# A decoder layer on one core: the first stage's work on two engines is given a written order, and three small pieces move

## The chip, the cores and the metric

One core of a Trainium2 chip runs the whole program. The metric is device time in microseconds (us) of one execution. The engines are TensorE (PE in the profile, its weight loads PEld), VectorE (DVE), ScalarE (ACT), GpSimd (POOL) and SyncE (SP), which issues most of the transfers.

## The reference, cut to what matters

One layer runs over 1024 prompt positions and 64 sample positions (T = 1088 columns here), with 1024 features. What the change touches is the beginning:

```python
h = rmsnorm(x, g1)              # x * rsqrt(mean(x*x) + EPS) * g1
proj = h @ w_in                 # 1024 x 2824
u, v, bgate, cgate, hb, z, xbc, dt_raw = jnp.split(proj, cuts, axis=-1)
conv_out, conv_new = causal_dwconv(cgate * hb, conv_prev, conv_w)
xbc_c, sconv_new = causal_dwconv(xbc, sconv_prev, sconv_w, sconv_b)   # then silu
dt = jax.nn.softplus(dt_raw + dt_bias)
```

Behind it come three token mixers, an output projection, and a feed-forward block of 4096 hidden features, `x + relu(rmsnorm(x) @ w_ff1)**2 @ w_ff2`, which is most of the matrix work.

## The kernel before

Features lie on the 128 partitions and tokens in the columns. `xT` is 8 tiles `xt` of 128 x 1088. Products are taken in float32r, with each operand split in a rounded part (high) and a rest (low); `mm3` (L125) adds high x high, low x high and high x low. A weight tile `whl` (128 x 2 x 1024) is made by `split_w` (L94) out of a loaded tile `wst`: ScalarE writes the high part (L97), VectorE the low part (L98). Both pools have two buffers, so the third weight tile takes the buffer of the first. `next_w` (L114) hands out tile i, splits tile i+1 and loads tile i+2.

The first stage goes over the 8 tiles `xt` as they land (L247). For each k, `dt_products` (L240) issues 12 small matmuls of `xt` with the eight dt columns of the weights, into the PSUM tile `psd`. Then the high part of x * g1 is written to `big` (L254 on ScalarE for k > 2, L256 on VectorE for the others), the low part by VectorE (L259), the square of `xt` by ScalarE (L229, `square`, in place but for k = 0), and the squares are summed into `ss` on VectorE (L233, `add_square`). TensorE runs the products of the first weight tile (L333, L337; `w0`) on these parts as they come, into three PSUM tiles `gps`, all that this pool has. The norm's factor 1/rms isn't known by then: it is multiplied onto the results afterwards.

When `w0` is done, ScalarE copies its three PSUM tiles to the buffer `buf` (L342) and `psd` to `dtT` (L344, L345). The second weight tile's products follow (L322, `gemm` with L128 to L130): its first third goes to a PSUM tile `aps` of another pool, so that it need not wait for those copies, and behind that third stands `rms_scale` (L155): three matmuls that sum `ss` over the partitions (L169), a logarithm and an exponential on ScalarE (L170, L174), and a Newton step on VectorE (L177 to L180) that gives `rstd`. Then VectorE multiplies the second tile's results by `rstd` (L290, `evac_pad`), the first tile's by `rstd` (L351), and `dtT` by `rstd` (L355, L357), and the convolutions follow (`conv_c`: L304 on ScalarE, three L307 on VectorE, L309 on ScalarE). Between the thirds of the third weight tile's products stand the small matmuls `dt_tokens` (L379) that turn `dtT` over.

Each engine works its own instructions in the order in which they stand in its program. That order is made by the framework's planner: it runs its own estimate of the program in time, and takes among the instructions that it holds for ready the one that was written first. Within `tc.manual_schedule(engines={...})` (used here at the end, L1346) the engines named keep to the written order instead; engines not named stay with the planner.

Of the kernel before, what the change touches and what calls it, by code (L numbers as in the profile page):

```python
# [7 lines left out]
F32 = mybir.dt.float32  # L8
F32R = mybir.dt.float32r
BF16 = mybir.dt.bfloat16  # L10
AF = mybir.ActivationFunctionType
ALU = mybir.AluOpType
# [3 lines left out]
P = 128  # L16
D = 1024
KT = D // P
# [4 lines left out]
T = SEQ + TS  # L23
# [36 lines left out]
HC = (0, 256, 1024)  # L60
# [8 lines left out]
def body(nc, tc, I, O):  # L69
    ctx = ExitStack()  # L70
    V, S, G, PE, SY = nc.vector, nc.scalar, nc.gpsimd, nc.tensor, nc.sync
# [11 lines left out]
    big = bigp.tile([P, KT * 2 * T], F32R, name="big")  # L83

    def C(name):
        o, n = PCOLS[name]
        return cp[:, o:o + n]
# [3 lines left out]
        SY.dma_start(out=st, in_=src)  # L91
        return st

    def split_w(st, cuts=(0, 1024), pool=None):  # L94
        w = (pool or whlp).tile([P, 2, 1024], F32R, name="whl")
        for a, b in zip(cuts, cuts[1:]):
            S.copy(out=w[:, 0, a:b], in_=st[:, a:b])  # L97
            V.tensor_tensor(out=w[:, 1, a:b], in0=st[:, a:b], in1=w[:, 0, a:b].bitcast(F32),  # L98
                            op=ALU.subtract)
        return w  # L100
# [5 lines left out]
    def w_load(i):  # L106
        if i < len(w_plan) and i not in w_st:
            w_st[i] = load_w(w_plan[i])

    def w_split(i):  # L110
        if i < len(w_plan) and i not in w_sp:
            w_sp[i] = split_w(w_st[i], HC if i == 0 else (0, 1024))

    def next_w():  # L114

# [111 lines left out]
    def square(k):  # L227
        xt = xts[k][:, :T]
        S.activation(out=ss if k == 0 else xt, in_=xt, func=AF.Square)  # L229

    def add_square(k):
        if k > 0:
            V.tensor_tensor(out=ss, in0=ss, in1=xts[k][:, :T], op=ALU.add)  # L233
# [6 lines left out]
    def dt_products(k):  # L240

        parts = [(j, 0, DTQ, j * DTQ) for j in range(4)] + [(j, DTQ, 32, SEQ + 32 * j) for j in range(2)]
        for j, o, n, t in parts:
            PE.matmul(psd[32 * j:32 * j + 32, o:o + n], wdt[:, k], xts[k][:, t:t + n],
                      start=k == 0 and o == 0, stop=k == KT - 1, skip_group_check=True)

    for k in range(KT):  # L247
        xt = xts[k]
        dt_products(k)
        b = big[:, k * 2 * T:(k + 1) * 2 * T].rearrange("p (h t) -> p h t", h=2)  # L250
        g = C("g1")[:, k:k + 1]
        for a, e in (((0, 364), (364, T)) if k == 0 else ((0, T),)):
            if k > 2:
                S.activation(out=b[:, 0, a:e], in_=xt[:, a:e], func=AF.Identity, scale=g)  # L254
            else:
                V.tensor_scalar(out=b[:, 0, a:e], in0=xt[:, a:e], scalar1=g, scalar2=None, op0=ALU.mult)  # L256
        if k == 0:
            w_split(0)
        V.scalar_tensor_tensor(out=b[:, 1], in0=xt[:, :T], scalar=g, in1=b[:, 0].bitcast(F32),  # L259
                               op0=ALU.mult, op1=ALU.subtract)  # L260
        if k:
            square(k - 1)
        if k > 2:
            add_square(k - 2)
        xg.append(b)
    w_split(1)
    square(KT - 1)
    add_square(KT - 2)
    add_square(KT - 1)

    def evac_mul(c, ps, dst, rhs=None):
        rhs = rstd if rhs is None else rhs
# [3 lines left out]
    def pad_parts(buf, pad, src, c):  # L276

        c0, n = CH[c]
        if c < 2:
            return [(buf[:, pad + c0:pad + c0 + n], src[:, :n], lambda a: a[:, c0:c0 + n])]  # L280
        m, w = SEQ - c0, NJ + pad
        sb = buf[:, pad + SEQ:pad + SEQ + NB * w].rearrange("p (b w) -> p b w", w=w)
        rows = lambda a: a.rearrange("p (b w) -> p b w", w=NJ)
        return [(buf[:, pad + c0:pad + SEQ], src[:, :m], lambda a: a[:, c0:SEQ]),
                (sb[:, :, pad:], rows(src[:, m:n]), lambda a: rows(a[:, SEQ:T]))]
# [3 lines left out]
        for o, i, tok in pad_parts(buf, pad, ps, c):  # L289
            V.tensor_tensor(out=o, in0=i, in1=tok(rhs), op=ALU.mult)  # L290

    S.copy(out=ones, in_=C("ones"))
    stC = sml.tile([P, 8, 27], F32, name="stC")
    xcS = sml.tile([P, 8, TS], F32, name="xcS")
    mids = {}
# [44 lines left out]
    for c in range(3):  # L340
        for o, i, tok in pad_parts(buf, 3, ps0[c], c):
            S.copy(out=o, in_=i)  # L342
    dtT = tmpp.tile([P, T], F32, name="dtT", tag="t")[:, :DTQ + 32]
    S.copy(out=dtT[:, :DTQ], in_=psd[:, :DTQ])  # L344
    S.copy(out=dtT[:64, DTQ:], in_=psd[:64, DTQ:DTQ + 32])  # L345
    buf5 = new_buf(3, C("sst")[:, 5 * 24:6 * 24])
    gemm(next_w(), xg, range(KT), lambda c, ps: evac_pad(c, ps, buf5, 3),
         first=ap.tile([P, 512], F32, name="aps", tag="a"), hooks=[lambda: rms_scale(aslots(), catp, "yb", ss, rstd, D, False)])
    for c in range(3):
        for o, i, tok in pad_parts(buf, 3, ps0[c], c):  # L350
            V.tensor_tensor(out=o, in0=o, in1=tok(rstd), op=ALU.mult)  # L351
    conv_c(4, buf)
    for j in range(4):
        r = slice(32 * j, 32 * j + 32)
        V.tensor_tensor(out=dtT[r, :DTQ], in0=dtT[r, :DTQ], in1=rstd[r, j * DTQ:(j + 1) * DTQ], op=ALU.mult)  # L355
        if j < 2:
            V.tensor_tensor(out=dtT[r, DTQ:], in0=dtT[r, DTQ:], in1=rstd[r, SEQ + 32 * j:SEQ + 32 * j + 32],  # L357
                            op=ALU.mult)
    conv_c(5, buf5)


# [95 lines left out]

    stB = sml.tile([P, 2, 18], F32, name="stB")
    catB = []
    V.tensor_tensor(out=ss, in0=rstd, in1=rstd, op=ALU.mult)  # L460

    def proj_b(i):
        cg = tmpp.tile([P, T], F32, name="cg", tag="t")
# [1152 lines left out]
```

## Time and profile before

| | |
|---|---|
| median of 3 runs | 1127.13 us (1126.9 to 1127.19) |
| profiled execution, its own time | 1127.05 us |
| its span, first to last instruction | 1125.3 us |
| TensorE matmul busy | 1111.0 us, 99% of the span, 8524 matmuls |
| VectorE busy | 840.4 us, 75% |
| ScalarE busy | 497.8 us, 44% |
| GpSimd busy | 53.2 us, 5% |

Busy times are unions of the recorded spans of instructions. A matmul's recorded end is modelled, and neighbours overlap, so what a matmul costs is better read from start to start. An idle time in square brackets is what lies ahead of an instruction on its engine, with what ended it.

### The profile page before, as it was taken

Reading aid. Unit: us, or ns where it says so; the run is one execution under the profiler, and the core shown is the slowest. Engines: PE = TensorE matmul, PEld = TensorE weight load, DVE = VectorE, ACT = ScalarE, POOL = GpSimd, SP = SyncE. Lnnn points to the kernel's source line nnn. Section 1 sums busy time; section 2 is a strip of 40 time slices with the busy share of each in tenths; the row PEclk is TensorE's granted clock in tenths of the full one; section 3 lists DMA queues with packets and bytes.
Section 4 is the critical chain, followed back from the end, with each engine's and each line's share of the span. In section 5 each row is a group of like instructions: output and inputs, shape, how many; then the busy total and the mean of one; then the engine's idle time right before and its main releaser. Section 6 shows DMA issues by size and latency. Waiting matters only on the chain.

```text
span 1125.3 us, 19943 instructions
## 1 busy us (share of the span) xinstructions
PE 1111.0 (99%) x8524; PEld 1090.8 (97%) x8524; DVE 840.4 (75%) x1111; ACT 497.8 (44%) x659; POOL 53.2 (5%) x89
## 2 busy tenths in 40 slices
PE   8999999999999999999999999999999999999996
PEld 6999999999999999999999999999999999999995
DVE  8875587865655477999697497596596596599786
ACT  7536273423553344653343443443443442543544
POOL 1110021110000000000000000000000000000014
PEclk9999999999999999999999999999999999999999
DMA  6112233321027263692853953953953953953504
GB/s 257 52 60 62 61 113 104 114 70 52 34 93 280 79 229 117 277 410 80 336 175 129 399 180 138 390 185 138 394 180 144 382 186 146 378 183 142 215 1 160
DMA packets 34776, 200.43 MB, mean 178 GB/s; under 512 B 4736, under 2 KB 7680, under 8 KB 27776
## 3 DMA queue, kind: packets, MB, share of 16 engines
q1 hardware_dynamic: 32592, 196.30, 47.2%
q10 hardware_dynamic: 2096, 2.85, 0.7%
q8 instruction: 67, 1.10, 0.4%
q14 instruction: 21, 0.17, 0.0%
HBM read 175.58 MB, written 22.77 MB: 176 GB/s over the span
## 4 chain that ended last, share of the span: by engine, by line
PE 94%; DVE 3%; issue 1%; ACT 1%; DMA 1%; POOL 0%; SPq 0%; POOLq 0%; DVEq 0%; ACTq 0%
PE ps L1045 20%; PE ps L1044 20%; PE ps L1046 20%; PE gps L128 10%; PE gps L129 9%; PE gps L130 9%; PE aps L574 1%; PE aps L578 1%; DMA xt<-xT 1%; DVE big L259 1%; DVE xq L909 0%; PE aps L509 0%; PE aps L505 0%; PE p L1044 0%; PE aps L767 0%
## 5 line engine op out<-in xcount | busy, mean ns | idle before, releaser
L1045 PE MATMUL ps<-big,whl 128*128 128x272 f32 x1312 | 377.7, 288 | 0.0
L1044 PE MATMUL ps<-big,whl 128*128 128x272 f32 x1312 | 377.5, 288 | 0.0
L1046 PE MATMUL ps<-big,whl 128*128 128x272 f32 x1312 | 376.9, 287 | 0.0
L1045 PEld LDWEIGHTS ps<-big,whl 128*128 128x128 f32 x1312 | 247.1, 188 | 0.2 <-issue 0.2
L1044 PEld LDWEIGHTS ps<-big,whl 128*128 128x128 f32 x1312 | 247.1, 188 | 0.2
L1046 PEld LDWEIGHTS ps<-big,whl 128*128 128x128 f32 x1312 | 246.8, 188 | 0.0
L128 PE MATMUL gps<-big,whl 128*128 128x360 f32 (+2 forms) x752 | 239.8, 319 | 0.5 <-ACT cb L342 0.5
L129 PE MATMUL gps<-big,whl 128*128 128x360 f32 (+2 forms) x752 | 236.8, 315 | 0.5 <-DVE whl L98 0.5
L130 PE MATMUL gps<-big,whl 128*128 128x360 f32 (+2 forms) x752 | 236.0, 314 | 0.0
L97 ACT CAST whl<-wq 128x1024 fp32r<-128x1024 f32 x92 | 96.6, 1051 | 220.7 <-PE ps L1046 132.9
L98 DVE TENSOR_TENSOR whl<-wq,whl 128x1024 fp32r<-128x1024 f32 x92 | 112.3, 1220 | 50.1 <-ACT whl L97 50.1
L128 PEld LDWEIGHTS gps<-big,whl 128*128 128x128 f32 x752 | 141.4, 188 | 2.0 <-ACT cb L342 1.0
L129 PEld LDWEIGHTS gps<-big,whl 128*128 128x128 f32 x752 | 141.4, 188 | 1.1 <-DVE whl L98 0.7
L130 PEld LDWEIGHTS gps<-big,whl 128*128 128x128 f32 x752 | 141.3, 188 | 0.1
L944 DVE TENSOR_TENSOR x<-x,ps 128x544 f32<-128x544 f32 x188 | 130.5, 713 | 7.8 <-PE ps L1046 6.7
L1046 PE MATMUL ps<-fo,whl 128*128 128x272 f32 x416 | 119.5, 287 | 0.0
L1044 PE MATMUL ps<-fo,whl 128*128 128x272 f32 x416 | 119.3, 287 | 0.0
L1045 PE MATMUL ps<-fo,whl 128*128 128x272 f32 x416 | 119.2, 287 | 0.0
L97 ACT CAST whl<-wst 128x1024 fp32r<-128x1024 f32 (+2 forms) x39 | 40.1, 1027 | 129.5 <-PE gps L130 81.0
L1044 PEld LDWEIGHTS ps<-fo,whl 128*128 128x128 f32 x416 | 78.3, 188 | 0.2 <-issue 0.2
L1046 PEld LDWEIGHTS ps<-fo,whl 128*128 128x128 f32 x416 | 78.2, 188 | 0.0
L1045 PEld LDWEIGHTS ps<-fo,whl 128*128 128x128 f32 x416 | 78.2, 188 | 0.0
(327 smaller groups left out, 1382.1 us busy)
## 6 DMA issues: line engine op xcount, KB each, us to landing
big<-xcd SPq DMA_DIRECT2D x47, 2176.0 KB, 9.7
wq<-w SPq DMA_DIRECT2D x66, 512.0 KB, 4.5
xcd<-big SPq DMA_DIRECT2D x7, 2176.0 KB, 8.1
wst<-w_in SPq DMA_DIRECT2D x21, 512.0 KB, 3.6
wst<-w_out SPq DMA_DIRECT2D x16, 512.0 KB, 3.6
x<-xT SPq DMA_DIRECT2D x8, 544.0 KB, 5.4
dec<-scr SPq DMA_DIRECT2D x8, 512.0 KB, 4.1
xt<-xT SPq DMA_DIRECT2D x7, 544.0 KB, 9.0
```

What stands on the lines that cost most here:

```text
L97: S.copy(out=w[:, 0, a:b], in_=st[:, a:b])
L98: V.tensor_tensor(out=w[:, 1, a:b], in0=st[:, a:b], in1=w[:, 0, a:b].bitcast(F32), op=ALU.subtract)
L128: PE.matmul(ps[:, :n], hi, xh, start=start, stop=False)
L129: PE.matmul(ps[:, :n], lo, xh, start=False, stop=False)
L130: PE.matmul(ps[:, :n], hi, xl, start=False, stop=stop)
L259: V.scalar_tensor_tensor(out=b[:, 1], in0=xt[:, :T], scalar=g, in1=b[:, 0].bitcast(F32), op0=ALU.mult, op1=ALU.subtract)
L574: PE.matmul(yps[hh * HD:(hh + 1) * HD, i * L:(i + 1) * L], w[:, h * HD:(h + 1) * HD], m[:, h], start=i == 0 and n == 0, stop=n == len(term ...
L578: PE.matmul(sps[:, g * 256:(g + 1) * 256], bt[:, g * P:(g + 1) * P], xw[:, g * 256:(g + 1) * 256], start=True, stop=True)
L944: V.tensor_tensor(out=out, in0=a, in1=b, op=o)
L1044: PE.matmul(o, hi, xh, start=start and k == 0, stop=False, skip_group_check=True)
L1045: PE.matmul(o, lo, xh, start=False, stop=False, skip_group_check=True)
L1046: PE.matmul(o, hi, xl, start=False, stop=k == ks - 1, skip_group_check=True)
```

## The change

The loop over k becomes three functions, `high`, `low` and the old `square`/`add_square`, called from one block in which VectorE and ScalarE keep to the written order; TensorE, GpSimd and SyncE stay with the planner. Within the block all sums of squares but the first (which is a write) stand behind the last low part, the split of the second weight tile stands behind the first of these sums, and at the end of the block come the load and the split of the third weight tile and the two copies of `psd` to `dtT`. The first weight tile is split in the same two pieces as before, at written places. The copy of `ones` moves behind the first tile's PSUM copies. `dtT` times `rstd` moves ahead of the first tile's multiplication by `rstd` and its convolution. `ss = rstd * rstd`, which is first read by the products of mixer B (L274), moves from VectorE to ScalarE as a Square.

```diff
@@ -91,8 +91,9 @@
         SY.dma_start(out=st, in_=src)
         return st
 
-    def split_w(st, cuts=(0, 1024), pool=None):
-        w = (pool or whlp).tile([P, 2, 1024], F32R, name="whl")
+    def split_w(st, cuts=(0, 1024), pool=None, w=None):
+        if w is None:
+            w = (pool or whlp).tile([P, 2, 1024], F32R, name="whl")
         for a, b in zip(cuts, cuts[1:]):
             S.copy(out=w[:, 0, a:b], in_=st[:, a:b])
             V.tensor_tensor(out=w[:, 1, a:b], in0=st[:, a:b], in1=w[:, 0, a:b].bitcast(F32),
@@ -109,7 +110,7 @@
 
     def w_split(i):
         if i < len(w_plan) and i not in w_sp:
-            w_sp[i] = split_w(w_st[i], HC if i == 0 else (0, 1024))
+            w_sp[i] = split_w(w_st[i])
 
     def next_w():
 
@@ -245,28 +246,52 @@
                       start=k == 0 and o == 0, stop=k == KT - 1, skip_group_check=True)
 
     for k in range(KT):
-        xt = xts[k]
-        dt_products(k)
-        b = big[:, k * 2 * T:(k + 1) * 2 * T].rearrange("p (h t) -> p h t", h=2)
+        xg.append(big[:, k * 2 * T:(k + 1) * 2 * T].rearrange("p (h t) -> p h t", h=2))
+
+    def high(k):
         g = C("g1")[:, k:k + 1]
         for a, e in (((0, 364), (364, T)) if k == 0 else ((0, T),)):
+            o, i = xg[k][:, 0, a:e], xts[k][:, a:e]
             if k > 2:
-                S.activation(out=b[:, 0, a:e], in_=xt[:, a:e], func=AF.Identity, scale=g)
+                S.activation(out=o, in_=i, func=AF.Identity, scale=g)
             else:
-                V.tensor_scalar(out=b[:, 0, a:e], in0=xt[:, a:e], scalar1=g, scalar2=None, op0=ALU.mult)
-        if k == 0:
-            w_split(0)
-        V.scalar_tensor_tensor(out=b[:, 1], in0=xt[:, :T], scalar=g, in1=b[:, 0].bitcast(F32),
-                               op0=ALU.mult, op1=ALU.subtract)
-        if k:
-            square(k - 1)
-        if k > 2:
-            add_square(k - 2)
-        xg.append(b)
-    w_split(1)
-    square(KT - 1)
-    add_square(KT - 2)
-    add_square(KT - 1)
+                V.tensor_scalar(out=o, in0=i, scalar1=g, scalar2=None, op0=ALU.mult)
+
+    def low(k):
+        V.scalar_tensor_tensor(out=xg[k][:, 1], in0=xts[k][:, :T], scalar=C("g1")[:, k:k + 1],
+                               in1=xg[k][:, 0].bitcast(F32), op0=ALU.mult, op1=ALU.subtract)
+
+
+    ET = mybir.EngineType
+    with tc.manual_schedule(engines={ET.DVE, ET.Activation}):
+        for k in range(KT):
+            dt_products(k)
+        high(0)
+        low(0)
+        w_sp[0] = whlp.tile([P, 2, 1024], F32R, name="whl")
+        split_w(st0, HC[:2], w=w_sp[0])
+        square(0)
+        high(1)
+        low(1)
+        split_w(st0, HC[1:], w=w_sp[0])
+        high(2)
+        square(1)
+        low(2)
+        for k in range(3, KT):
+            high(k)
+            low(k)
+        add_square(1)
+        square(2)
+        w_split(1)
+        for k in range(2, KT):
+            if k > 2:
+                square(k)
+            add_square(k)
+        w_load(2)
+        w_split(2)
+        dtT = tmpp.tile([P, T], F32, name="dtT", tag="t")[:, :DTQ + 32]
+        S.copy(out=dtT[:, :DTQ], in_=psd[:, :DTQ])
+        S.copy(out=dtT[:64, DTQ:], in_=psd[:64, DTQ:DTQ + 32])
 
     def evac_mul(c, ps, dst, rhs=None):
         rhs = rstd if rhs is None else rhs
@@ -289,7 +314,6 @@
         for o, i, tok in pad_parts(buf, pad, ps, c):
             V.tensor_tensor(out=o, in0=i, in1=tok(rhs), op=ALU.mult)
 
-    S.copy(out=ones, in_=C("ones"))
     stC = sml.tile([P, 8, 27], F32, name="stC")
     xcS = sml.tile([P, 8, TS], F32, name="xcS")
     mids = {}
@@ -340,22 +364,20 @@
     for c in range(3):
         for o, i, tok in pad_parts(buf, 3, ps0[c], c):
             S.copy(out=o, in_=i)
-    dtT = tmpp.tile([P, T], F32, name="dtT", tag="t")[:, :DTQ + 32]
-    S.copy(out=dtT[:, :DTQ], in_=psd[:, :DTQ])
-    S.copy(out=dtT[:64, DTQ:], in_=psd[:64, DTQ:DTQ + 32])
+    S.copy(out=ones, in_=C("ones"))
     buf5 = new_buf(3, C("sst")[:, 5 * 24:6 * 24])
     gemm(next_w(), xg, range(KT), lambda c, ps: evac_pad(c, ps, buf5, 3),
          first=ap.tile([P, 512], F32, name="aps", tag="a"), hooks=[lambda: rms_scale(aslots(), catp, "yb", ss, rstd, D, False)])
-    for c in range(3):
-        for o, i, tok in pad_parts(buf, 3, ps0[c], c):
-            V.tensor_tensor(out=o, in0=o, in1=tok(rstd), op=ALU.mult)
-    conv_c(4, buf)
     for j in range(4):
         r = slice(32 * j, 32 * j + 32)
         V.tensor_tensor(out=dtT[r, :DTQ], in0=dtT[r, :DTQ], in1=rstd[r, j * DTQ:(j + 1) * DTQ], op=ALU.mult)
         if j < 2:
             V.tensor_tensor(out=dtT[r, DTQ:], in0=dtT[r, DTQ:], in1=rstd[r, SEQ + 32 * j:SEQ + 32 * j + 32],
                             op=ALU.mult)
+    for c in range(3):
+        for o, i, tok in pad_parts(buf, 3, ps0[c], c):
+            V.tensor_tensor(out=o, in0=o, in1=tok(rstd), op=ALU.mult)
+    conv_c(4, buf)
     conv_c(5, buf5)
 
 
@@ -457,7 +479,7 @@
 
     stB = sml.tile([P, 2, 18], F32, name="stB")
     catB = []
-    V.tensor_tensor(out=ss, in0=rstd, in1=rstd, op=ALU.mult)
+    S.activation(out=ss, in_=rstd, func=AF.Square)
 
     def proj_b(i):
         cg = tmpp.tile([P, T], F32, name="cg", tag="t")
```

## Rows read from the trace of the kernel before

**Rows 1.** The page: busy time of TensorE and its weight loads, VectorE, ScalarE, GpSimd (share of the span, instructions), and the chain of work that ended last, by engine.

```profile
PE 1111.0 (99%) x8524; PEld 1090.8 (97%) x8524; DVE 840.4 (75%) x1111; ACT 497.8 (44%) x659; POOL 53.2 (5%) x89
PE 94%; DVE 3%; issue 1%; ACT 1%; DMA 1%; POOL 0%; SPq 0%; POOLq 0%; DVEq 0%; ACTq 0%
```

**Rows 2.** Busy time of the engines in stretches of the span: stretch, its length, then busy time and instructions by engine, the granted clock of TensorE, the share of DMA time and GB/s.

```profile
8.06:25.11 17.05, 17.05 (x154) 14.09 (x154) 16.91 (x15) 14.78 (x15) 2.28 (x2) 1.00 0.76 305
25.11:26.75 1.64, 1.11 (x4) 0.39 (x4) 1.64 (x3) 1.64 (x6) 0.00 (x0) 1.00 0.00 0
56.00:1100.00 1044.00, 1043.51 (x7991) 1032.36 (x7990) 777.27 (x1008) 451.91 (x591) 32.63 (x54) 1.00 0.49 179
```

**Rows 3.** What TensorE's matmuls waited for over the whole execution: us in total, times, longest us.

```profile
PE aps L244 <- DMA xt<-xT: 1.7, 1, 1.7
...
PE gps L128 <- ACT cb L342: 0.5, 1, 0.5
...
PE aps L379 <- DVE dtT L355: 0.2, 1, 0.2
```

**Rows 4.** TensorE in order of time around the end of the first weight tile: start us, us, instruction, count, idle time ahead of it.

```profile
24.61 0.66 PE L333 MATMUL gps<-big,whl 128*128 128x364 f32 x3
25.11 0.33 PE L128 MATMUL aps<-big,whl 128*128 128x364 f32 x1
25.97 0.80 PE L128 MATMUL gps<-big,whl 128*128 128x364 f32 x2 [0.53 <-ACT cb L342]
26.75 0.43 PE L129 MATMUL aps<-big,whl 128*128 128x364 f32 x1
...
30.69 1.99 PE L169 MATMUL aps<-ss,cp 128*128 128x364 f32 x6
```

**Rows 5.** TensorE in order of time around the small matmuls on `dtT`.

```profile
43.99 0.33 PE L130 MATMUL gps<-big,whl 128*128 128x364 f32 x1
44.56 0.83 PE L379 MATMUL aps<-cp,dtT 128*128 128x8 f32 x6 [0.23 <-DVE dtT L355]
...
54.51 0.43 PE L128 MATMUL gps<-big,whl 128*128 128x364 f32 x1
```

**Rows 6.** VectorE in order of time in the first stage.

```profile
11.70 1.28 DVE L233 TENSOR_TENSOR ss<-ss,xt 128x1088 f32<-128x1088 f32 x1
12.90 3.86 DVE L259 SCALAR_TENSOR_TENSOR big<-xt,cp,big 128x1088 fp32r<-128x1088 f32 x3
...
23.02 1.34 DVE L259 SCALAR_TENSOR_TENSOR big<-xt,cp,big 128x1088 fp32r<-128x1088 f32 x1
...
25.49 1.21 DVE L98 TENSOR_TENSOR whl<-wst,whl 128x1024 fp32r<-128x1024 f32 x1
26.62 2.67 DVE L233 TENSOR_TENSOR ss<-ss,xt 128x1088 f32<-128x1088 f32 x2
29.21 1.22 DVE L98 TENSOR_TENSOR whl<-wst,whl 128x1024 fp32r<-128x1024 f32 x1
```

**Rows 7.** ScalarE in order of time in the first stage.

```profile
11.79 2.50 ACT L254 ACTIVATE big<-xt,cp 128x1088 fp32r<-128x1088 f32 x2 [0.38 <-DMA xt<-xT]
...
23.01 1.03 ACT L97 CAST whl<-wst 128x1024 fp32r<-128x1024 f32 x1
...
24.45 1.12 ACT L229 ACTIVATE xt<-xt 128x1088 f32<-128x1088 f32 x1 [0.21 <-DVE big L259]
25.47 1.24 ACT L342 COPY cb<-gps 128x364 f32<-128x364 f32 x4
26.57 0.41 ACT L344 COPY dtT<-aps 128x256 f32<-128x256 f32 x1
...
28.10 1.28 ACT L170 ACT_TABLE_LOAD   x1
```

**Rows 8.** Transfers: SyncE's issue of the second weight tile, and for all loads of `wst` up to 60 us the time from issue to landing.

```profile
8.04 0.33 SPq L91 DMA_DIRECT2D wst<-w_in  x1
DMA to landing us min/median/max: 3.3/3.9/10.3
```

**Rows 9.** The norm's factor and what VectorE does with it, in order of time.

```profile
31.50 1.78 ACT L170 ACTIVATE rt<-aps,cp 128x364 f32<-128x364 f32 x3 [2.12 <-PE aps L169]
...
40.21 0.53 DVE L180 SCALAR_TENSOR_TENSOR rstd<-rt,rstd 128x360 f32<-128x360 f32 x1
40.65 1.36 DVE L351 TENSOR_TENSOR cb<-cb,rstd 128x364 f32<-128x364 f32 x3
...
42.56 0.40 DVE L355 TENSOR_TENSOR dtT<-dtT,rstd 32x256 f32<-32x256 f32 x1
...
44.53 7.81 DVE L307 SCALAR_TENSOR_TENSOR xc<-cb,cp,xc 128x1112 f32<-128x1112 f32 x6
52.27 1.22 DVE L98 TENSOR_TENSOR whl<-wst,whl 128x1024 fp32r<-128x1024 f32 x1
53.40 0.97 DVE L290 TENSOR_TENSOR cb<-gps,rstd 128x364 f32<-128x364 f32 x2
```

**Rows 10.** `ss` from `rstd` on VectorE, and its first reader.

```profile
55.34 1.27 DVE L460 TENSOR_TENSOR ss<-rstd 128x1088 f32<-128x1088 f32 x1
121.61 0.53 DVE L274 TENSOR_TENSOR cg<-gps,ss 128x364 f32<-128x364 f32 x1
```

## The prediction, made before the changed kernel was run

> **What bounds the kernel now.** I read the page first, to see which engine the end hangs on: matmuls fill 99% of the span and TensorE holds 94% of the chain that ended last [rows 1]. VectorE at 75% and ScalarE at 44% matter only where TensorE waits for them. Next the table by stretches: from 56 to 1100 us TensorE is idle for 0.49 us of 1044, at the full granted clock of 1.00, that is 2.4 GHz [rows 2]. So an edit that makes VectorE or ScalarE quicker there is worth next to nothing, and the change must earn its time ahead of 56 us, where all of its parts but one lie.
>
> The list of TensorE's waits then says what there is to earn [rows 3]. Three of its entries lie ahead of 56 us and behind the warm-up: 1.7 us for the second `xt` (up to 8.06 us), 0.5 us for the first tile's PSUM copy, 0.2 us for `dtT`. From 8.06 to 25.11 us TensorE has 17.05 us busy of 17.05 [rows 2]: the first weight tile's products are limited by TensorE itself, not by the two engines whose order is now written down. What the waits cost is read from start to start in the timeline. Three matmuls of 364 columns take from 24.61 to 25.11 us, 0.167 us each [rows 4]. At that pace the three L128 from 25.11 us would be followed at 25.61 us; the next one, L129, starts at 26.75 us. **Stall 1 is 1.14 us**: 0.53 us for L342, whose first copy starts at 25.47 us [rows 7], and the rest for the low part of the second weight tile, which VectorE writes from 25.49 to 26.70 us [rows 6] because it stands behind the sums of squares. The second: L130 starts at 43.99, the next should at 44.16 and does at 44.56 us [rows 5]. **Stall 2 is 0.40 us**, for `dtT` times `rstd`, which ends at 44.5 us, just ahead of L307 [rows 9].
>
> **The change part by part.**
>
> *The order on VectorE.* The same instructions run, so their sum stays. Before, low parts alternate with sums from 11.70 us on, and the last low part ends at 23.02 + 1.34 = 24.36 us [rows 6]. Now six low parts follow one another at 3.86 / 3 = 1.29 us. Starting where the first sum stood, 11.70 + 6 x 1.29 gives 19.4 us. They may also be held by transfers: between 8.06 and 11.79 us there landed 0.39 MB of the first weight tile and two `xt` of 0.56 MB [rows 3, 7], 1.38 us for one `xt`, so the eighth lands at 11.79 + 4 x 1.38 = 17.3, its high part ends at 18.5 (half of 2.50 us on ScalarE, [rows 7]) and its low part at 19.9 us. Then one sum (1.2 to 1.3 us) and the second weight tile's low part (1.21 us), which so ends at 22 to 22.4 instead of 26.70 us, some 2.8 us ahead of its first use at 25.3 us. The 1.14 us of stall 1 go. For TensorE in the first tile nothing is won by earlier low parts, since it was never waiting for one.
>
> The last sum: VectorE was without a gap from 11.70 to 30.4 us and the third tile's low part is last before and after, so `ss` is complete at 26.62 + 2.67 = 29.29 us as before, up to 0.4 later where transfers hold it [rows 6]. TensorE will be through the first third of the second tile at 25.11 + 24 x 0.167 = 29.11 us and then wants `ss` for L169 (before: 30.69 us, 1.4 us behind `ss`, [rows 4]). What was cover is now a wait of 0.2 us; bounds 0 (the planner puts other matmuls ahead) and 0.6. I take 0.2.
>
> *The order on ScalarE.* High parts first, at the pace of the landings, to 18.5 us. Then a square (1.12), the second tile's cast (1.03; its load, issued at 8.04 us, lands after at most 10.3 us, at 18.3 us [rows 8]), five squares: 18.5 + 1.1 + 1.0 + 5 x 1.1 = 26.1 us, against 24.45 + 1.12 = 25.57 us before [rows 7]. The last square is needed by the last sum at 28 us: 1.9 us of cover. Behind it now stands the third tile's cast, to 27.1 us. It waits for the first tile's buffer, which TensorE frees at 25.1 to 25.4 us, so that wait is over. Then the copies to `dtT` (0.34 us from start to start), 27.5 us, and only then the four PSUM copies L342, that were done at 26.57: now at 28.6 us. TensorE wants the first of these tiles behind L169, at 29.1 + 1.6 = 30.7 us; 2 us of cover, and if that fails it is the slower rival below. The table load of 1.28 us ends at 29.9 us, and the logarithm can't start ahead of 29.3 + 0.8 us (31.50 against 30.69 before, [rows 4, 9]): no cost.
>
> *`dtT` ahead of the first tile.* The norm's chain starts 1.1 to 1.4 us earlier, so `rstd`, complete at 40.7 us before [rows 9], comes at 39.4. The six small products take 44.5 - 42.56 = 2.0 us, and 1 us of the second tile's results (two L290 at 0.97 us for two, [rows 9]) may go ahead: 42.4 us at the latest. TensorE arrives at 44.16 - 1.14 + 0.2 = 43.2 us. Stall 2's 0.40 us go, with 0.8 us to spare.
>
> What is late next: the third L290 group at 53.40 us, which frees the PSUM tile that TensorE takes up again at 54.51 us [rows 5, 9]. It ended at 53.9, so it had 0.6 us. TensorE comes 1.3 to 1.5 us earlier, VectorE's queue up to there (without a gap from 40.21 us) 1.1 to 1.4 us earlier. Cost 0 if so; 1.3 us at most less, if VectorE has to stand still for one L304 because the first tile's results are ready 2 us later in the queue. The bound is thus 0 to 0.9 us; I take 0.1, since the other convolution's L307 can go first.
>
> *The rest at nothing.* `ss` from `rstd` takes 1.27 us off VectorE at 55 us [rows 10] and puts about 1.1 us (a Square of the same size, [rows 7]) on ScalarE; it is read at 121.61 us, and TensorE waits for neither engine in that stretch. The earlier load of the third weight tile has the same buffer to wait for. `ones` is not wanted before the later norm. Should the Square need a table of its own, two loads of 1.28 us on an engine idle 56% of the time would be hidden as well.
>
> Sum, against the profiled execution's 1127.05 us (span 1125.3, 1.75 around it; the median is 1127.13): 1127.05 - 1.14 - 0.40 + 0.2 + 0.1 = 1125.8. Against the median that is 1125.9; I give **1125.8 us**, 0.12% faster. A measurement of this kernel tells about 0.2%, 2.25 us, from no change, so my forecast is "same".
>
> **The strict order of ScalarE, weighed.** The timeline shows ScalarE's instructions one after another, L342 ended before L344 [rows 7]; whether one could pass a waiting one is not seen there. The Trainium skill, "TensorE: Matmul & The Clock Gate", section on the architectural detail of the array, states that ScalarE and VectorE take their queues strictly first in, first out, while TensorE may pull weight loads ahead. By that rule all that stands behind the third tile's cast waits with it, which is the slower rival; by a queue that lets them pass, that rival would be void. The row neither confirms nor denies it.
>
> **The rivals.**
> *Forecast (0.56):* both stalls go, with givebacks of 0 to 0.6 us: 1125.4 to 1126.2.
> *One gain is given back (0.18):* the wait for `ss` at its 0.6 us or the PSUM tile at 54.5 us at 0.9 us. 1127.05 - 1.54 + 0.9 = 1126.4, with both 1127.0. For it: slacks of 0.2 and 0.6 us are small. Against: both queues move together.
> *Slower: the third tile's cast holds up the PSUM copies (0.10).* If the planner again puts two `gps` matmuls ahead of L129, TensorE in its own order waits for L342, whose first two copies now end at about 28.0 and 28.4 instead of 25.97 and 26.3 us. L129 would start at 28.5 instead of 26.75: 1.75 us lost, 0.40 won, 1128.4 us. It passes the 0.2% when ScalarE's squares run another 1 us later, as when the second tile's load lands 2 us late. For it: that order stands in the trace of before [rows 4]. Against: it was then natural, since the low part came after the copies; now it comes 2.8 us ahead. I put half of this chance beyond 0.2%.
> *The planner's order moves elsewhere (0.16):* TensorE is not in the written block, and its order, and that of everything behind, follows from the planner's own estimate of the new times. Faster than 2.25 us can't come from the two stalls together (1.54 us); it would need 0.7 us from such a shift: 0.12 for faster, 0.04 for slower.
>
> **How the numbers follow.** Faster 0.12; slower 0.05 + 0.04 = 0.09; the rest, 0.79, within 0.2%. The range runs from a small lucky shift, 1124.6, to the held-up copies with part of their price, 1128.2.
>
> **What would show it.** Right: no wait of TensorE for L342 or L98 between 25 and 27 us; L98 of the second tile near 21 us; the first L169 at 29.1 to 29.7 us; no idle time ahead of the first L379. Wrong: `gps` matmuls waiting for L342 near 28 us; an idle TensorE at 53 us for L290; gaps on TensorE between 8 and 25 us, which would mean that the written order starves it.

## The result, and the profile after

The changed kernel takes 1128.51 us (median of 21 runs, 1127.86 to 1130.15) against 1126.87 us for the kernel before on the same chips (21 runs): a ratio of 1.0015, interval [1.0009, 1.002]. It is slower by 1.6 us (0.15%) where 1.3 us faster (0.12%) was forecast, and lies above the range's 1128.2. That is less than the 0.2% from which a difference was to count, so "same" came out as forecast; but the interval leaves out 1, and the sign is wrong.

The page of the changed kernel's profile (its own time 1128.27 us, span 1126.5) has the lines that answer to [rows 1]:

```profile
PE 1112.1 (99%) x8524; PEld 1092.4 (97%) x8524; DVE 839.8 (75%) x1110; ACT 498.7 (44%) x660; POOL 48.7 (4%) x89
PE 95%; DVE 2%; ACT 1%; issue 1%; DMA 1%; POOL 0%; SPq 0%; POOLq 0%; DVEq 0%; ACTq 0%
```

They hardly differ. The list of what TensorE's matmuls waited for (us, times, longest) does, against [rows 3]:

```profile
PE aps L401 <- DVE dtT L373: 1.4, 1, 1.4
PE aps L245 <- DMA xt<-xT: 1.0, 1, 1.0
```

The wait for the copy of the first tile's PSUM tiles, into which the matmuls had written (L342), is gone, as forecast; that for `dtT` has grown from 0.2 to 1.4 us. TensorE in order of time, to be held against [rows 4, 5] (L129 to L131 are the old L128 to L130, L170 the old L169, L401 the old L379):

```profile
7.57 0.69 PE L245 MATMUL aps<-xt,wdt 128*32 128x256 f32 x12 [1.05 <-DMA xt<-xT]
...
24.10 0.66 PE L357 MATMUL gps<-big,whl 128*128 128x364 f32 x3
24.60 0.33 PE L129 MATMUL aps<-big,whl 128*128 128x364 f32 x1
24.77 0.33 PE L130 MATMUL aps<-big,whl 128*128 128x364 f32 x1
...
31.25 0.33 PE L130 MATMUL gps<-big,whl 128*128 128x364 f32 x1
31.41 1.99 PE L170 MATMUL aps<-ss,cp 128*128 128x364 f32 x6
...
42.15 0.33 PE L131 MATMUL gps<-big,whl 128*128 128x364 f32 x1
43.88 0.84 PE L401 MATMUL aps<-cp,dtT 128*128 128x8 f32 x6 [1.40 <-DVE dtT L373]
...
55.47 0.43 PE L129 MATMUL gps<-big,whl 128*128 128x364 f32 x1
```

Stall 1 is gone: L130 follows L129 after 0.17 us. But the first L170 stands at 31.41 us, behind 17 matmuls of the second third. Next to what it waits for that is late: VectorE in order of time, against [rows 6, 9] (L234 the sums of squares, L99 a weight tile's low part, L427 a small instruction of a later step, L181 the end of `rstd`, L373 `dtT`, L331 the convolutions, L315 the results times `rstd`):

```profile
11.32 7.89 DVE L261 SCALAR_TENSOR_TENSOR big<-xt,cp,big 128x1088 fp32r<-128x1088 f32 x6
19.13 1.28 DVE L234 TENSOR_TENSOR ss<-ss,xt 128x1088 f32<-128x1088 f32 x1
20.33 1.23 DVE L99 TENSOR_TENSOR whl<-wst,whl 128x1024 fp32r<-128x1024 f32 x1
21.48 6.88 DVE L234 TENSOR_TENSOR ss<-ss,xt 128x1088 f32<-128x1088 f32 x5
28.27 0.16 DVE L427 TENSOR_SCALAR na<-na 128x8 f32<-128x8 f32 x1
28.39 1.29 DVE L234 TENSOR_TENSOR ss<-ss,xt 128x1088 f32<-128x1088 f32 x1
...
40.93 0.52 DVE L181 SCALAR_TENSOR_TENSOR rstd<-rt,rstd 128x360 f32<-128x360 f32 x1
41.37 0.40 DVE L373 TENSOR_TENSOR dtT<-dtT,rstd 32x256 f32<-32x256 f32 x1
...
42.98 0.85 DVE L373 TENSOR_TENSOR dtT<-dtT,rstd 32x256 f32<-32x256 f32 x2
43.86 1.50 DVE L379 TENSOR_TENSOR cb<-cb,rstd 128x364 f32<-128x364 f32 x4
45.28 1.22 DVE L99 TENSOR_TENSOR whl<-wst,whl 128x1024 fp32r<-128x1024 f32 x1
46.80 7.81 DVE L331 SCALAR_TENSOR_TENSOR xc<-cb,cp,xc 128x1112 f32<-128x1112 f32 x6 [0.31 <-ACT xc L328]
54.54 0.97 DVE L315 TENSOR_TENSOR cb<-gps,rstd 128x364 f32<-128x364 f32 x2
```

`ss` is complete at 28.39 + 1.29 = 29.68 us, 1.73 us before L170 adds it up. `rstd` ends at 41.45 us (before: 40.74). The first L315 of the last pair shown, which frees a PSUM tile, ends at 55.1 us instead of 53.9, in a program whose TensorE had saved stall 1 by then.

There is one more thing in this trace. The table by stretches shows the granted clock (the column of 1.00, 0.99, 0.50, 0.97) at half, 1.2 GHz, for some three microseconds behind the stall:

```profile
0.00:44.00 44.00, 39.98 (x279) 33.14 (x280) 34.67 (x48) 28.01 (x34) 3.16 (x13) 1.00 0.50 187
44.00:46.00 2.00, 2.00 (x15) 2.00 (x16) 2.00 (x5) 0.55 (x1) 0.72 (x1) 0.99 0.00 0
46.00:49.00 3.00, 3.00 (x11) 3.00 (x11) 2.69 (x3) 1.98 (x2) 0.68 (x2) 0.50 0.37 139
49.00:56.00 7.00, 7.00 (x48) 6.96 (x48) 6.92 (x10) 0.93 (x1) 1.45 (x4) 0.97 0.04 15
```

There a matmul takes 0.303 us from start to start instead of 0.167; over the 11 of that stretch 1.5 us. My first theory was therefore: late `rstd`, a stall of 1.56 us (from start to start) in place of 0.40, stall 1 saved, and some 1.5 us by the fall of the clock: 1.56 + 1.5 - 0.40 - 1.14 = 1.5 us, about the 1.64 us measured. The experiments took the second half of it away.

To compare executions, times are best counted from the landing of the second `xt`, which differs between executions of any of these programs (7.21 to 8.47 us), while what follows repeats within 0.1 us. In the table each number is the time of an instruction less the start of the second group of dt products, which waits for that landing (8.06 us before, 7.57 us changed). "L315 (L290) done" is the end of the first instruction of the pair, which frees the PSUM tile; the rows below the first three are the experiments of the next section:

| kernel | `ss` done | first sum L170 | `rstd` done | `dtT` done | L315 (L290) done | 4th weight tile starts | end |
|---|---|---|---|---|---|---|---|
| before | 21.23 | 22.62 | 32.67 | 36.44 | 45.87 | 46.45 | 1117.20 |
| changed | 22.11 | 23.84 | 33.88 | 36.26 | 47.50 | 47.90 | 1118.92 |
| changed, once more | 22.07 | 23.85 | 33.89 | 36.26 | 47.50 | 47.65 | 1118.96 |
| tokens later | 22.08 | 23.84 | 33.89 | 36.27 | 47.51 | 47.66 | 1120.13 |
| sums first | 22.10 | 22.15 | 32.30 | 34.13 | 45.89 | 46.03 | 1117.04 |
| sums behind nine | 22.08 | 22.53 | 32.57 | 34.94 | 46.18 | 46.33 | 1117.39 |
| stall longer | 21.24 | 22.63 | 32.68 | 37.64 | 47.07 | 49.09 | 1119.83 |
| dt first alone | 21.24 | 22.63 | 32.68 | 35.14 | 47.19 | 47.33 | 1118.14 |
| dt behind | 22.08 | 23.90 | 33.94 | 37.69 | 47.12 | 47.27 | 1118.31 |
| `ss` on VectorE | 22.08 | 23.84 | 33.88 | 36.26 | 48.30 | 48.45 | 1119.42 |
| own PSUM tile | 22.05 | 23.84 | 33.89 | 36.26 | 47.50 | 46.34 | 1117.35 |
| tokens later, own PSUM tile | 22.10 | 23.85 | 33.89 | 36.26 | 47.50 | 44.67 | 1115.65 |
| before, the same two | 21.29 | 22.69 | 32.73 | 36.50 | 45.93 | 46.07 | 1116.78 |

### The profile page after: what moved, and what is told of

It reads as the page before. It is cut to its first block, busy times and chain, and to the rows that moved or that the text cites. A ratio compares the mean times of both kernels' runs of the same rounds, so it can differ in the third digit from the quotient of the medians.

```text
span 1126.5 us, 19949 instructions
## 1 busy us (share of the span) xinstructions
PE 1112.1 (99%) x8524; PEld 1092.4 (97%) x8524; DVE 839.8 (75%) x1110; ACT 498.7 (44%) x660; POOL 48.7 (4%) x89
## 4 chain that ended last, share of the span: by engine, by line
PE 95%; DVE 2%; ACT 1%; issue 1%; DMA 1%; POOL 0%; SPq 0%; POOLq 0%; DVEq 0%; ACTq 0%
PE ps L1067 20%; PE ps L1066 20%; PE ps L1068 20%; PE gps L129 10%; PE gps L130 9%; PE gps L131 9%; PE aps L596 1%; PE aps L600 1%; PE gps L357 1%; DMA xt<-xT 1%; DVE xq L931 0%; PE gps L361 0%; PE aps L245 0%; PE aps L531 0%; PE aps L527 0%
## 5 line engine op out<-in xcount | busy, mean ns | idle before, releaser
L129 PE MATMUL gps<-big,whl 128*128 128x360 f32 (+2 forms) x752 | 240.4, 320 | 0.0
L130 PE MATMUL gps<-big,whl 128*128 128x360 f32 (+2 forms) x752 | 237.1, 316 | 0.5 <-DVE whl L99 0.5
L131 PE MATMUL gps<-big,whl 128*128 128x360 f32 (+2 forms) x752 | 237.0, 315 | 0.0
L98 ACT CAST whl<-wq 128x1024 fp32r<-128x1024 f32 x92 | 96.6, 1051 | 220.7 <-PE ps L1068 133.0
L99 DVE TENSOR_TENSOR whl<-wq,whl 128x1024 fp32r<-128x1024 f32 x92 | 112.2, 1220 | 50.9 <-ACT whl L98 50.9
L129 PEld LDWEIGHTS gps<-big,whl 128*128 128x128 f32 x752 | 142.0, 189 | 1.1 <-issue 0.2
L130 PEld LDWEIGHTS gps<-big,whl 128*128 128x128 f32 x752 | 142.0, 189 | 0.9 <-DVE whl L99 0.7
L131 PEld LDWEIGHTS gps<-big,whl 128*128 128x128 f32 x752 | 141.8, 189 | 0.1
L98 ACT CAST whl<-wst 128x1024 fp32r<-128x1024 f32 (+2 forms) x39 | 40.0, 1027 | 128.8 <-PE gps L131 80.6
```

Source lines behind the costliest of these rows:

```text
L129: PE.matmul(ps[:, :n], hi, xh, start=start, stop=False)
L130: PE.matmul(ps[:, :n], lo, xh, start=False, stop=False)
L131: PE.matmul(ps[:, :n], hi, xl, start=False, stop=stop)
```

## The experiments

**The changed kernel once more**, with nothing but an empty line added at its end.

> The changed kernel itself once more, on the same chip as the others. Theory: the stall of about 1.4 us idle ahead of L401 and the fall of the clock from about 46 us on come in this execution too, 1128.5 us. Rival (the fall is a chance of one execution): no fall of the clock at 46 us, and 1127.0 us in it.

Measured 1128.58 us (11 runs), ratio 1.0013 [1.0004, 1.0022]. TensorE in this execution, and the clock in the stretch:

```profile
43.58 0.83 PE L401 MATMUL aps<-cp,dtT 128*128 128x8 f32 x6 [1.40 <-DVE dtT L373]
...
54.91 0.40 PE L129 MATMUL gps<-big,whl 128*128 128x364 f32 x1 [1.31 <-DVE cb L315]
```

The table by stretches of the same execution, with the granted clock near the end of each line:

```profile
44.00:56.00 12.00, 10.69 (x73) 10.61 (x73) 11.69 (x18) 5.37 (x5) 2.85 (x6) 1.00 0.14 45
```

The same stall ahead of L401, and no fall of the clock: the fall comes in one execution of this program and not in another. But the time is not 1.5 us less. In its place there is a second wait, 1.38 us from start to start, ahead of the fourth weight tile, for L315. That is the forecast's own sign of being wrong, an idle TensorE waiting for L290 (now L315). In the first execution TensorE came some 1.6 us later to that place, nearly all of it by the clock, and needn't wait. So VectorE sets a floor under both: L315 ends 47.50 us after the second `xt` in each, and the fourth tile can't start before 47.65 us (in the kernel before it started at 46.45). The first execution, at 47.90, lies 0.25 us above that floor.

**The small matmuls one third later.**

```diff
-    for i, hooks in ((6, [lambda: dt_tokens((0, 1, 2)), lambda: dt_tokens((3, 4, 5)), softplus]), (7, ()), (0, ()), (1, [cumsums]), (2, ()), (3, ())):
+    for i, hooks in ((6, [lambda: None, lambda: dt_tokens((0, 1, 2)), lambda: (dt_tokens((3, 4, 5)), softplus())]), (7, ()), (0, ()), (1, [cumsums]), (2, ()), (3, ())):
```

> The changed kernel with the three groups of small matmuls on dtT one third of a weight tile later; VectorE's and ScalarE's orders stay. Theory (the stall ahead of the first L401, 1.57 us, and behind it 3.4 us at 1.2 GHz, 1.54 us, make the loss): TensorE arrives some 4 us later, dtT is ready, both go: about 1125.4 us, 0.13% faster than before. Rival A (the fall of the clock has another cause than this stall): the stall goes, the fall stays, about 1126.9 us. Rival B (the time lost lies elsewhere, in the order behind 56 us): about 1128.5 us.

Measured 1130.31 us (9 runs), ratio 1.0027 [1.0017, 1.0036]: slower than any of the three expected. All of TensorE's waits between 9 and 100 us:

```profile
PE gps L129 <- DVE cb L315: 2.9, 1, 2.9
```

The stall ahead of the small matmuls is gone, and both stalls are now one at L315, which ends where it did. The stall for `dtT` was no loss of its own. And behind this wait the clock fell, to 0.50 from 57 to 59 us, with no wait behind it that would hide it. This execution starts the fourth tile when the changed kernel once more does and ends 1.2 us behind it; the medians lie 1.7 us apart, and the other 0.5 us one trace doesn't show.

**TensorE's order for the second weight tile written, the sums right behind the first third.**

```diff
-    gemm(next_w(), xg, range(KT), lambda c, ps: evac_pad(c, ps, buf5, 3),
-         first=ap.tile([P, 512], F32, name="aps", tag="a"), hooks=[lambda: rms_scale(aslots(), catp, "yb", ss, rstd, D, False)])
+    w5 = next_w()
+    with tc.manual_schedule(engines={ET.PE}):
+        gemm(w5, xg, range(KT), lambda c, ps: evac_pad(c, ps, buf5, 3),
+             first=ap.tile([P, 512], F32, name="aps", tag="a"), hooks=[lambda: rms_scale(aslots(), catp, "yb", ss, rstd, D, False)])
```

> The changed kernel with TensorE's matmuls of the second weight tile in the written order, so that L170 stands right behind the first third (28.6 us) instead of behind 17 matmuls of the second third (31.4 us). Theory (rstd is late because the planner put L170 late): L170 waits until ss is complete, at 29.7 us, 1.1 us lost there, rstd comes 1.7 us earlier, the stall ahead of the small matmuls goes and the fall of the clock with it: about 1126.5 us. Rival (any stall of this length brings the fall of the clock): 1128.0 us.

Measured 1126.61 us (11 runs), ratio 0.9995 [0.9986, 1.0004]. The wait is there, and it is the only one between 9 and 100 us:

```profile
28.42 0.33 PE L131 MATMUL aps<-big,whl 128*128 128x364 f32 x1
29.55 0.88 PE L170 MATMUL aps<-ss,cp 128*128 128x364 f32 x2 [0.81 <-DVE ss L234]
```

`rstd` is 1.6 us earlier than in the changed kernel, L315 as well, and no stall is left at either place. The loss goes with the late L170. What was forecast doesn't come even so: with L170 where the prediction had it, TensorE waits 0.97 us for `ss` (from start to start), where 0.2 was taken and 0.6 was the bound.

**The sums behind nine matmuls of the second third.**

```diff
-    gemm(next_w(), xg, range(KT), lambda c, ps: evac_pad(c, ps, buf5, 3),
-         first=ap.tile([P, 512], F32, name="aps", tag="a"), hooks=[lambda: rms_scale(aslots(), catp, "yb", ss, rstd, D, False)])
+    w5 = next_w()
+    with tc.manual_schedule(engines={ET.PE}):
+        p50 = ap.tile([P, 512], F32, name="aps", tag="a")
+        for k in range(KT):
+            mm3(p50, w5, k, xg[k], *CH[0], k == 0, k == KT - 1)
+        p51 = gp.tile([P, 512], F32, name="gps", tag="g")
+        for k in range(3):
+            mm3(p51, w5, k, xg[k], *CH[1], k == 0, False)
+        rms_scale(aslots(), catp, "yb", ss, rstd, D, False)
+        evac_pad(0, p50, buf5, 3)
+        for k in range(3, KT):
+            mm3(p51, w5, k, xg[k], *CH[1], False, k == KT - 1)
...
```

> The changed kernel with TensorE's matmuls of the second weight tile in a written order in which L170 stands behind nine matmuls of the second third, some 30.1 us: behind ss (29.7 us), so that TensorE doesn't wait for it. New theory (from 41 to 55 us VectorE's queue, which starts with rstd, sets when the PSUM tile of the third weight tile's first third is free at L315; what TensorE saves ahead of it, it waits there): L170 is 0.55 us later than in the run with the sums right behind the first third, so L315 is too, TensorE waits about 1.1 us ahead of the first L129 near 53.7 us, about 1127.1 us in all. Rival (each of TensorE's waits counts by itself): the wait of 0.97 us ahead of L170 goes and none comes, 1125.6 us.

Measured 1127.28 us (11 runs), ratio 1.0003 [0.9994, 1.0012], against 1127.1 expected by the new theory and 1125.6 by the rival.

```profile
54.18 0.41 PE L129 MATMUL gps<-big,whl 128*128 128x364 f32 x1 [1.24 <-DVE cb L315]
```

TensorE no longer waits for `ss`, wins 0.97 us there, and waits 1.30 us for L315. The rival's time lies below the interval, which begins at 1126.3 us. Up to 55 us VectorE's queue sets the time; what TensorE wins ahead of it is given back at L315. In all kernels with the changed order of VectorE's instructions behind `rstd` and `ss` on ScalarE, L315 is done 13.6 us behind `rstd`, wherever TensorE's waits lie (before: 13.2).

**The stall made longer in the kernel before.**

```diff
+    idle = catp.tile([P, T], F32, name="idle", tag="yb")
+    V.tensor_tensor(out=idle, in0=rstd, in1=rstd, op=ALU.mult)
     for c in range(3):
         for o, i, tok in pad_parts(buf, 3, ps0[c], c):
```

> The kernel before with one more VectorE instruction (1.27 us, rstd squared into a tile that nothing reads) ahead of the first tile's last multiplications, so that dtT comes 1.27 us later: the stall ahead of L379 grows from 0.40 to 1.67 us, no written order is involved. Theory (a stall of this length is followed by a fall of the clock): 1126.9 + 1.27 + 1.54 = 1129.7 us, with the granted clock at half for some 3.4 us about 2 us behind the stall. Rival (the fall belongs to the written order, not to the stall): 1128.1 us and no fall of the clock at 46 us.

Measured 1128.98 us (11 runs, 1127.94 to 1129.88), ratio 1.0015 [1.0007, 1.0024]. The profiled execution (1129.88 us) has the wait and the fall:

```profile
PE aps L381 <- DVE dtT L357: 1.3, 1, 1.3
```

The table by stretches, around the fall of the clock behind that wait:

```profile
47.00:48.00 1.00, 1.00 (x6) 1.00 (x5) 1.00 (x2) 0.98 (x1) 0.00 (x0) 0.67 0.00 0
48.00:50.00 2.00, 2.00 (x8) 2.00 (x8) 2.00 (x3) 0.00 (x0) 0.00 (x0) 0.50 0.00 0
```

So the fall needs no written order; it came behind a stall of this kind without one. Counted from the second `xt`, this execution ends 2.63 us behind the kernel before: `dtT` is 1.20 us later, and the other 1.4 us come with the clock. The times of the 11 runs go from one expectation to the other, as if the fall didn't follow always; that is read from the times, not from a second trace.

**dt first, alone:** the kernel before, with the six products of `dtT` moved ahead of the first tile's multiplication.

```diff
+    for j in range(4):
+        r = slice(32 * j, 32 * j + 32)
+        V.tensor_tensor(out=dtT[r, :DTQ], in0=dtT[r, :DTQ], in1=rstd[r, j * DTQ:(j + 1) * DTQ], op=ALU.mult)
...
     for c in range(3):
         for o, i, tok in pad_parts(buf, 3, ps0[c], c):
             V.tensor_tensor(out=o, in0=o, in1=tok(rstd), op=ALU.mult)
     conv_c(4, buf)
-    for j in range(4):
-        r = slice(32 * j, 32 * j + 32)
-        V.tensor_tensor(out=dtT[r, :DTQ], in0=dtT[r, :DTQ], in1=rstd[r, j * DTQ:(j + 1) * DTQ], op=ALU.mult)
...
```

> The kernel before with one part of the change alone: dtT times rstd ahead of the first tile's multiplication. New theory: dtT is ready at 42.8 us, the stall of 0.40 us at 44.2 us goes; but the first tile's results come 2 us later, VectorE waits 0.3 us for L304 as it does in the changed kernel, L290 frees its PSUM tile at about 54.3 us, and TensorE, which arrives at 54.1, waits 0.2 us there: 1126.7 us. Rival (the saving stays): 1126.5 us; rival (this part is what makes the change slower): 1128 us or more, with a wait of over 1 us ahead of L128 near 55 us.

Measured 1127.96 us (11 runs), ratio 1.001 [1.0002, 1.0019]: slower, by the time of the third expectation. VectorE in order of time:

```profile
45.06 1.22 DVE L98 TENSOR_TENSOR whl<-wst,whl 128x1024 fp32r<-128x1024 f32 x1
46.19 1.29 DVE L460 TENSOR_TENSOR ss<-rstd 128x1088 f32<-128x1088 f32 x1
47.39 7.81 DVE L307 SCALAR_TENSOR_TENSOR xc<-cb,cp,xc 128x1112 f32<-128x1112 f32 x6
55.12 0.98 DVE L290 TENSOR_TENSOR cb<-gps,rstd 128x364 f32<-128x364 f32 x2
```

And what TensorE waited for in that kernel, beside stall 1, which is as before:

```profile
PE gps L128 <- DVE cb L290: 1.3, 1, 1.3
```

The stall for `dtT` goes, but the first tile's results come 2 us later, ScalarE can't begin the convolutions, and the planner fills VectorE's wait with L460, which then runs into the time when the convolutions could start. From `rstd` to the end of L290 it is 14.5 us instead of 13.2.

**dt behind, in the changed kernel.**

```diff
-    for j in range(4):
-        r = slice(32 * j, 32 * j + 32)
-        V.tensor_tensor(out=dtT[r, :DTQ], in0=dtT[r, :DTQ], in1=rstd[r, j * DTQ:(j + 1) * DTQ], op=ALU.mult)
...
     for c in range(3):
         for o, i, tok in pad_parts(buf, 3, ps0[c], c):
             V.tensor_tensor(out=o, in0=o, in1=tok(rstd), op=ALU.mult)
     conv_c(4, buf)
+    for j in range(4):
+        r = slice(32 * j, 32 * j + 32)
+        V.tensor_tensor(out=dtT[r, :DTQ], in0=dtT[r, :DTQ], in1=rstd[r, j * DTQ:(j + 1) * DTQ], op=ALU.mult)
...
```

> The changed kernel with one part undone: dtT times rstd behind the first tile's multiplication and its convolution, as before. New theory: dtT is ready near 45.2 us, TensorE waits some 2.9 us ahead of L401 instead of 1.57; L315 frees its PSUM tile at about 54.5 us as in the changed kernel, and TensorE arrives there at 54.8 us without waiting: the same 1128.5 us where the clock doesn't fall, up to 1130.0 us where it falls behind the longer stall. Rival (the stall ahead of L401 is the loss, one for one): 1129.8 us without a fall of the clock.

Measured 1128.06 us (11 runs), ratio 1.0014 [1.0005, 1.0023]; its interval and that of the changed kernel overlap. The waits:

```profile
PE aps L401 <- DVE dtT L377: 1.3, 1, 1.3
PE gps L129 <- DVE cb L315: 0.9, 1, 0.9
```

I had expected one wait of 2.9 us: the planner moved the small matmuls back by nine of the third tile's (the last matmul ahead of them starts 1.55 us later from the second `xt`, at 0.167 us each), so it came in two parts, 1.45 and 0.98 us. L315 ends 0.4 us earlier than in the changed kernel (47.12 against 47.50), since VectorE needn't stand still ahead of the convolutions. The move of `dtT`, meant for the stall of 0.40 us, is worth nothing there; this execution without it even ends 0.6 us earlier.

**`ss` on VectorE, in the changed kernel.**

```diff
-    S.activation(out=ss, in_=rstd, func=AF.Square)
+    V.tensor_tensor(out=ss, in0=rstd, in1=rstd, op=ALU.mult)
```

> The changed kernel with one part undone: ss = rstd * rstd on VectorE as before. It stands there (1.27 us) ahead of the six L331, where VectorE is idle for 0.31 us. New theory (VectorE's queue from rstd to L315 sets the time): L315 comes 0.95 us later and TensorE waits that much longer ahead of the fourth weight tile: 1129.4 us. Rival (this part is hidden, as was predicted): 1128.5 us.

Measured 1130.64 us (5 runs), ratio 1.0034 [1.0021, 1.0046]. In the trace L315 ends 48.30 us after the second `xt`, 0.80 us later than in the changed kernel, as expected to 0.15 us. The median is 2.1 us above the changed kernel's, 1.2 us more than expected. The one trace (1129.83 us, the fastest of the five, with a fall of the clock) ends 0.5 us behind the changed kernel's, counted from the second `xt`; where the rest lies it doesn't show, and that stays open.

**The fourth tile's first third in a PSUM tile of the other pool.**

```diff
-        gemm(next_w(), xg, range(KT), lambda c, ps: evac_pad(c, ps, buf, 3), hooks)
+        gemm(next_w(), xg, range(KT), lambda c, ps: evac_pad(c, ps, buf, 3), hooks,
+             first=ap.tile([P, 512], F32, name="aps", tag="a") if i == 7 else None)
```

> The changed kernel with the fourth weight tile's first third in a PSUM tile of the other pool, the small matmuls on dtT where they are. New theory: the stall of 1.57 us ahead of L401 stays, the wait for L315 near 55 us goes, 1127.1 us where the clock doesn't fall behind the stall; where it falls, nothing covers it any more and it costs 1.5 us, 1128.6 us. Rival (the PSUM tile is not what VectorE's queue delays): 1128.5 us with a wait of over 1 us near 55 us.

Measured 1128.06 us (11 runs), ratio 1.001 [1.0001, 1.0019]. The profiled execution took 1126.96 us, at a clock of 1.00 from 44 to 56 us, with one wait:

```profile
PE aps L402 <- DVE dtT L374: 1.4, 1, 1.4
```

The runs fall into two groups, 1126.75 to 1127.41 us (five) and 1128.06 to 1129.37 (six), as the two expectations have it: nothing waits at L315 any more, so a fall of the clock would show in the time. That the clock is what parts the two groups is argued; no execution of the slower one was traced.

**Both ways closed, in the changed kernel and in the kernel before.** The small matmuls one third later and the fourth tile's own PSUM tile, as above, together.

> The changed kernel with the groups of small matmuls on dtT one third of a tile later (no wait for dtT) and with the fourth weight tile's first third in a PSUM tile of the other pool, so that it doesn't wait for L315. New theory (VectorE's late queue reaches TensorE by these two ways alone): neither the stall ahead of L401 nor that at 55 us, no fall of the clock, 1125.4 us. Rival (a third thing is late as well, such as the low part of a weight tile or the next PSUM tile): a wait of over 1 us between 52 and 62 us, 1126.9 us or more.

> The kernel before with the two reliefs that made the changed kernel fastest: the small matmuls on dtT one third later, and the fourth weight tile's first third in a PSUM tile of the other pool. New theory: the stall of 0.40 us ahead of L379 goes, the stall of 1.14 us behind the first weight tile stays, no PSUM tile was waited for: 1126.6 us, 1 us above the changed kernel with the same reliefs. Rival (the written order in itself saves nothing): both at 1125.6 us.

The changed kernel with both takes 1125.59 us (11 runs), ratio 0.999 [0.9982, 0.9999], faster than both kernels; TensorE waits for nothing between 9 and 100 us. Counted from the second `xt`, it starts the fourth tile 1.78 us ahead of the kernel before and ends 1.55 us ahead of it. The kernel before with both takes 1126.58 us, 0.9998 [0.9989, 1.0006], with stall 1 left:

```profile
PE gps L128 <- ACT cb L343: 0.6, 1, 0.6
```

The two differ by 1.40 us at the start of the fourth tile, by 1.13 us at the end, and by 1.0 us in their medians, which come from two chips and whose intervals overlap. That is what the written order saves, stall 1 above all, once VectorE's delay can't reach TensorE.

The table holds a loss that no part of the sum had. From the start of the fourth tile to the end it is 1070.7 to 1070.8 us with the old order and 1071.0 to 1071.3 us with the written one ("tokens later" apart, where the clock falls in this stretch). In every traced execution with the written order, and in none of the others, a small matmul of the last norm (L892, before L870) some 13 us ahead of the end starts 0.2 us later against those ahead of it. Why is not shown. So it is in part chance that the 1.55 us equal the 1.14 + 0.40 of the prediction.

## Why the prediction was wrong

*Stall 1 (1.14 us): right.* The second tile's low part was written by 21.56 us, TensorE went on without a gap, and the two kernels with both ways closed differ by 1.13 us at the end. ScalarE did as forecast or better: its last square ended at 24.77 us (forecast 26.1), the PSUM copies were done at 27.3 us (28.6), so the rival of the held-up copies did not happen.

*`ss` as before, up to 0.4 later: mis-sized.* Counted from the second `xt` it came 0.88 us later. I had the same instructions give the same sum, but what a sum of squares takes hangs on what follows it. In both traces the next instruction starts 1.38 to 1.40 us after it where it is another sum, which reads the `ss` just written, and 1.20 to 1.21 us after it where it is not. Before, two sums of seven were followed by a sum; each of the others was followed by an instruction that doesn't read `ss`, as here (by L98 at 25.49 us, [rows 6]):

```profile
24.28 1.28 DVE L233 TENSOR_TENSOR ss<-ss,xt 128x1088 f32<-128x1088 f32 x1
```

Now four are, which makes 0.4 us of the 0.88; L427, placed ahead of the last sum, makes 0.1, and the rest, 0.3 to 0.4, came ahead of the sums, where the six low parts took 0.2 us longer.

*The step that failed: "bounds 0 (the planner puts other matmuls ahead)".* I priced other matmuls ahead of L169 at nothing, because TensorE loses nothing by them, and did not follow what waits for it. The planner put 17 matmuls of the second third ahead, L170 came at 31.41 us (the sign of being right was 29.1 to 29.7), 1.73 us behind a complete `ss`, and `rstd`, forecast 1.1 to 1.4 us earlier, came 0.71 us later, 1.21 counted from the second `xt`. The two runs with TensorE's order written show that this is the cause: with L170 1.7 and 1.3 us earlier, `rstd` and L315 are earlier by 1.6 and 1.3 us, and the times are 1126.6 and 1127.3 us. Why the planner's own estimate held `ss` for so late is not shown.

*Stall 2 (0.40 us): wrong.* `dtT` was ready at 43.83 us, forecast 42.4 at the latest, and TensorE came at 42.3, forecast 43.2. The stall grew to 1.56 us.

*The PSUM tile, "0 to 0.9, I take 0.1": the place was right, the size wrong.* The rival of the gain given back named this place, with a slack of 0.6 us and both queues moving together. They moved apart: TensorE ahead by stall 1, VectorE 1.2 us back with `rstd` and 0.4 more between `rstd` and L315, where the `dtT` products now stand ahead of the first tile's results (with them behind, in "dt behind", the way is 13.2 us again). That is 1.63 us at L315. Of the slack only 0.43 us counted, since TensorE starts 0.15 us behind L315; so the fourth tile starts 1.20 us later, at the floor of 47.65 us. Had I put `rstd`'s delay into that line, it would have given the slower result. Beyond these 1.20 us the two traces lose another 0.5 and 0.6 us: in the first 0.25 by the fall of the clock, the rest behind the start of the fourth tile, most of it in the last norm.

*`ss` on ScalarE at nothing: wrong in the changed order.* VectorE's queue between 41 and 55 us had no slack left, and with the instruction back on VectorE L315 is 0.80 us later.

*The fall of the clock* was in no part of the sum. It came behind the stall in one of the two traced executions, and in the changed kernel it costs little, 0.25 us at the fourth tile, since TensorE would have waited for L315 anyway.

## What to carry to other kernels

A saving on the engine that bounds the kernel is kept only if what that engine next needs comes earlier by as much, or has the slack to spare; so for each stall that goes, find the next buffer or operand that it takes up, and move the instruction that starts its producer's chain first. Where one engine's order is left to a planner, its new place for a small instruction with a long chain behind it (here three matmuls of 1.5 us) matters more than the gaps it fills.

## What the runs showed of the hardware

Two stalls of the same 1.40 us idle, in two executions of one program, were followed once by 3 us at half the granted clock (1.2 GHz) and once not. The second `xt` landed between 7.21 and 8.47 us in executions that had issued the same transfers up to there, which alone spreads the times by about 1 us; what follows repeated to 0.1 us. On VectorE the same sum of 128 x 1088 took 1.38 to 1.40 us from start to start where the next instruction read its result, and 1.20 to 1.21 us where it didn't.
